# A sparse 3x3 convolution on one core: all input loads issued at the start, every output pair stored in two halves

## The chip, the cores and the metric

The kernel runs on one core of a Trainium2 chip. The metric is the device time of one execution, in microseconds (us); lower is better. The time before is 126.25 us, the median of three runs.

## The reference

The reference is a 3x3 convolution with padding 1 over 16 images. Nine tenths of the weights are zero, but the kernel treats them as dense.

```python
x:      (16, 64, 64, 64)  float32      # batch, c_in, h, w
weight: (128, 64, 3, 3)   float32      # about 90% zeros
x_pad = np.pad(x, ((0,0),(0,0),(1,1),(1,1)))
for b, co, ci, kh, kw:
    output[b, co] += weight[co, ci, kh, kw] * x_pad[b, ci, kh:kh+64, kw:kw+64]
output: (16, 128, 64, 64) float32
```

The input is 16.8 MB, the output 33.6 MB.

## The kernel before, in words

**Pairs.** Images are worked on two at a time. A pair's 2 x 64 input channels fill the 128 partitions of a tile `x{p}` in bf16; there are eight such tiles, one for each pair p = 0 to 7, and none is reused. The loads are issued by GpSimd (the POOL queue), whose DMAs turn fp32 into bf16 on the way (L63 and L68). Only the first 32 rows of pair 0 (`x_head`) come as fp32 through SyncE's queue (L62) and are cast by VectorE and ScalarE (L101). The weights (`w_sb`, L60) come first on that queue.

**When the loads are issued.** Pair 0's second half, pairs 1 to 3 and the first 24 rows of pair 4 are issued at the start. The rest of pair 4 is issued when pair 1's last block has been summed, pair 5 after pair 2, pair 6 after pair 3, and pair 7 in two pieces of 32 rows after pairs 4 and 5 (table `LATER`, L74, calls L197 and L199). Since they stand in GpSimd's own order, they come between its row sums `s` (L169).

**The arithmetic.** Each block is 16 rows of a pair. `direct` (around L164; pair 0's first block alone) uses all nine taps for each row. `twos` takes two rows at a time: GpSimd adds neighbouring rows into `s` (L169), TensorE makes one shared product of `s`, which ScalarE copies out of PSUM into `pc` (L176), and two more products for even and odd rows, to which VectorE adds `pc` while it writes the output tile `o` (L183). All products are matmuls of L150, and a `twos` block has 30 of them.

**The output.** A pair's output is one fp32 tile of 128 partitions x 2 images x 64 rows x 64 columns, 4.2 MB, from a pool `o` of three buffers. SyncE stores a whole pair once its four blocks are written (L207). The last pair alone goes out in two halves of 32 rows (L205). A fourth pair needs the buffer of the first: VectorE's first write to pair p+3 waits until the store of pair p has landed.

**SyncE's eight semaphores.** The DMAs that SyncE issues take eight landing semaphores in turn. An issue whose semaphore was used by an earlier DMA waits until that DMA has landed, and everything behind it in SyncE's order waits too. Five loads of one element (`spare`, L211), issued after pair 1's store, move this rotation on.

In this text 0a and 0b are the first and second 32 rows of pair 0, and so on to 7b.

Of the kernel before, what the change touches and what calls it, by code (L numbers as in the profile page):

```python
# [8 lines left out]
FP32 = mybir.dt.float32  # L9
# [2 lines left out]
SUB = mybir.AluOpType.subtract  # L12

BLOCKS = {p: "TTTT" for p in range(8)}
BLOCKS[0] = "DTTT"  # L20


G0, G1, G2, G21, G01 = range(5)
# [4 lines left out]
def kernel(  # L28
# [6 lines left out]
    nc = tc.nc  # L35

    B, C_IN, H, W = x.shape
    C_OUT, _, KH, KW = weight.shape
    assert (B, C_IN, H, W) == (16, 64, 64, 64) and (C_OUT, KH, KW) == (128, 3, 3)
    NP = B // 2  # L40
    HEAD = 32

    const_pool = ctx.enter_context(tc.tile_pool(name="const", bufs=1))
    x_pool = ctx.enter_context(tc.tile_pool(name="x", bufs=1))
    s_pool = ctx.enter_context(tc.tile_pool(name="s", bufs=3))
    p_pool = ctx.enter_context(tc.tile_pool(name="pc", bufs=4))
    o_pool = ctx.enter_context(tc.tile_pool(name="o", bufs=3))
    psum_pool = ctx.enter_context(
        tc.tile_pool(name="psum", bufs=8, space=bass.MemoryType.PSUM)
    )  # L50
# [4 lines left out]
    def pair(p):  # L55
        return x[2 * p : 2 * p + 2].rearrange("n i h w -> (n i) h w")

    xs = [x_pool.tile([128, H, W], BF16, name=f"x{p}") for p in range(NP)]
# [5 lines left out]
    ident = const_pool.tile([128, 128], BF16, name="ident")  # L64
    make_identity(nc, ident)

    def load(p, a=0, b=H):
        nc.gpsimd.dma_start(out=xs[p][:, a:b, :], in_=pair(p)[:, a:b, :])  # L68

    EARLY, CUT = 4, 24

    LATER = {2: (5,), 3: (6,), 4: (7, 0, 32), 5: (7, 32, 64)}  # L74
    for p in range(1, EARLY):
        load(p)
    load(EARLY, 0, CUT)


    idle_rhs = const_pool.tile([128, 512], BF16, name="idle_rhs")  # L80
    nc.vector.memset(idle_rhs, 0.0)  # L81
# [2 lines left out]
    def keep_busy(n):  # L84
        for _ in range(n):
            nc.tensor.matmul(idle_ps, idle_rhs[:, 0:128], idle_rhs, start=True, stop=True)  # L86

    keep_busy(7)

    w_v = w_sb.rearrange("o (i k) -> o k i", k=KH * KW)
# [66 lines left out]
    def direct(p, o, r0, rows):  # L159
        ps = product(  # L160
            [(xs[p], G1, r0, 1), (xs[p], G0, r0 - 1, 1), (xs[p], G2, r0 + 1, 1)], rows
        )
        nc.scalar.copy(out=o[0][:, r0 : r0 + rows, :], in_=ps[0])  # L163
        nc.vector.tensor_copy(out=o[1][:, r0 : r0 + rows, :], in_=ps[1])  # L164

    def twos(p, o, r0):
        t0 = r0 // 2
        s = s_pool.tile([128, 8, W], BF16, name="s")
        nc.gpsimd.tensor_tensor(  # L169
            out=s, in0=xs[p][:, r0 : r0 + 16 : 2, :], in1=xs[p][:, r0 + 1 : r0 + 16 : 2, :], op=ADD  # L170
        )
        shared = product([(s, G1, 0, 1)], 8)
        pc = []
        for n in range(2):
            c = p_pool.tile([128, 8, W], FP32, name="pc")
            nc.scalar.copy(out=c, in_=shared[n])  # L176
            pc.append(c)
        even = [(xs[p], G21, r0 + 1, 2), (xs[p], G0, r0 - 1, 2)]
        odd = [(xs[p], G01, r0, 2), (xs[p], G2, r0 + 2, 2)]
        for first, terms in ((r0, even), (r0 + 1, odd)):  # L180
            ps = product(terms, 8)
            for n in range(2):
                nc.vector.tensor_tensor(  # L183
                    out=o[n][:, first : r0 + 16 : 2, :], in0=ps[n], in1=pc[n], op=ADD
                )

    for p in range(NP):
        both = o_pool.tile([C_OUT, 2, H, W], FP32, name="o")
        o = [both[:, n] for n in range(2)]
        into = out[2 * p : 2 * p + 2].rearrange("n o h w -> o n h w")  # L190
        last = p == NP - 1
        for blk in range(4):
            r0 = 16 * blk
            if BLOCKS[p][blk] == "T":
                twos(p, o, r0)
                if p == 1 and blk == 3:
                    load(EARLY, CUT, H)  # L197
                elif blk == 3 and p in LATER:
                    load(*LATER[p])  # L199
            else:  # L200
                for r, rows in ((r0, 8), (r0 + 8, 8)):
                    direct(p, o, r, rows)
            if last and blk % 2 == 1:
                rows = slice(r0 - 16, r0 + 16)
                nc.sync.dma_start(out=into[:, :, rows, :], in_=both[:, :, rows, :])  # L205
        if not last:
            nc.sync.dma_start(out=into, in_=both)  # L207
        if p == 1:
            spare = const_pool.tile([1, 5], FP32, name="spare")
            for k in range(5):  # L210
                nc.sync.dma_start(out=spare[:, k : k + 1], in_=weight[0:1, 0, 0, 0:1])  # L211


# [28 lines left out]
```

## Time and profile before

| | us |
|---|---|
| three runs | 125.86, 126.25, 126.41 |
| median | 126.25 |
| span of the profiled execution, first to last instruction | 124.3 |
| what the median has beyond that span | 1.95 |

The page gives the profiled execution by its span; no total of its own is listed beside it, so 1.95 us is taken as what lies around the span.

| engine | busy us | share of the span |
|---|---|---|
| TensorE (PE) | 108.7 | 87% |
| VectorE (DVE) | 82.5 | 66% |
| GpSimd (POOL) | 41.7 | 34% |
| ScalarE (ACT) | 39.0 | 31% |

The DMA share of a stretch is the mean busy share of the core's 16 DMA engines; it can come out a few hundredths above 1 where packets of an engine overlap. GB/s counts what is written at the destination, so a load that turns fp32 into bf16 counts with half of what it reads from HBM. Queue q0 (software) holds GpSimd's loads, queue q1 (hardware) what SyncE issues.

### The profile page before, as it was taken

To read this page: it belongs to the slowest core of one execution; us is meant where nothing else is said; L and a number is where in the kernel's file an instruction comes from. 1 tells how busy PE (TensorE), PEld (TensorE's weight loads), DVE (VectorE), ACT (ScalarE), POOL (GpSimd) and SP (SyncE) were. 2 spreads that over 40 slices of the span, in tenths; PEclk is the share of its full clock that TensorE was granted. 3 is DMA by queue.
4 is the path that set the end of the run, shared out by engine and by line. 5 is a ranking of instruction groups with operands and counts; after the bars stand their busy time and mean duration, and the time that the engine had idled before them with its cause. 6 is when DMAs were issued, how large, how long until landed. Compare 5 with 4: busy or idle time off the path is not lost.

```text
span 124.3 us, 2453 instructions
## 1 busy us (share of the span) xinstructions
PE 108.7 (87%) x989; PEld 57.2 (46%) x989; DVE 82.5 (66%) x135; ACT 39.0 (31%) x71; POOL 41.7 (34%) x47
## 2 busy tenths in 40 slices
PE   6959999999999999999999999999999999970000
PEld 2425555555555555555555555555555555530000
DVE  0353577877787778777877878887877787772000
ACT  4543333333333333333333333333333333330000
POOL 6409333533353335333443335333333320000000
PEclk9999999999999999999999999999999999997555
DMA  4999999999999999999999999999999999999991
GB/s 120 348 220 227 219 213 213 238 411 338 335 392 422 319 316 324 377 340 329 303 385 378 354 380 443 376 349 389 418 422 437 422 427 427 437 427 403 432 414 82
DMA packets 4198, 42.91 MB, mean 345 GB/s; under 512 B 347, under 2 KB 347, under 8 KB 1115
## 3 DMA queue, kind: packets, MB, share of 16 engines
q1 hardware_dynamic: 2746, 34.90, 67.2%
q0 software_dynamic: 1440, 7.86, 30.7%
q8 instruction: 7, 0.11, 0.3%
q14 instruction: 5, 0.03, 0.1%
HBM read 17.07 MB, written 33.55 MB: 407 GB/s over the span
## 4 chain that ended last, share of the span: by engine, by line
PE 82%; DMA 5%; DVE 1%; issue 1%; DVEq 0%; SPq 0%
PE ps L150 82%; DMA x_head<-in_x_dram 5%; DVE o L183 1%; DVEq L237 0%; DVE x L101 0%; SPq L60 0%; DVEq L183 0%
## 5 line engine op out<-in xcount | busy, mean ns | idle before, releaser
L183 DVE TENSOR_TENSOR o<-ps,pc 128x512 f32<-128x512 f32 x124 | 77.8, 686 | 22.1 <-PE ps L150 19.2
L150 PE MATMUL ps<-x,wT 64*128 64x504 bf16 (+3 forms) x780 | 88.8, 373 | 1.3 <-DVE x L101 1.3
L150 PEld LDWEIGHTS <-wT 64*128 64x128 bf16 x966 | 55.2, 94 | 49.5 <-issue 1.7
L169 POOL TENSOR_TENSOR s<-x 128x512 bf16<-128x512 bf16 x31 | 35.6, 1150 | 57.6 <-PE ps L150 41.1
L176 ACT COPY pc<-ps 128x512 f32<-128x512 f32 x62 | 33.3, 589 | 64.0 <-issue 61.8
L150 PE MATMUL ps<-s,wT 64*128 64x512 bf16 (+1 forms) x186 | 25.7, 377 | 0.0
L86 PE MATMUL ps<-idle_rhs 128*128 128x512 bf16 x14 | 4.8, 505 | 1.2 <-DVE idle_rhs L81 1.2
L68 POOL DMA_DIRECT2D x<-in_x_dram x9 | 5.0, 560 | 0.0
L86 PEld LDWEIGHTS <-idle_rhs 128*128 128x128 bf16 x14 | 1.5, 118 | 3.2 <-issue 1.4
L105 DVE CAST w_bf<-w_sb 128x192 bf16<-128x192 f32 (+1 forms) x4 | 1.1, 351 | 2.5 <-DMA w_sb<-in_weight_dram 2.5
L164 DVE COPY o<-ps 128x512 f32<-128x512 f32 x2 | 1.4, 692 | 2.0 <-PE ps L150 2.0
L101 DVE CAST x<-x_head 128x576 bf16<-128x576 f32 x1 | 0.5, 460 | 2.6 <-DMA x_head<-in_x_dram 2.6
L101 ACT CAST x<-x_head 128x576 bf16<-128x576 f32 (+1 forms) x2 | 1.5, 802 | 1.8 <-DMA x_head<-in_x_dram 1.8
L163 ACT COPY o<-ps 128x512 f32<-128x512 f32 x2 | 1.2, 586 | 2.4 <-PE ps L150 2.4
L105 ACT ACT_TABLE_LOAD x1 | 1.3, 1283 | 0.7 <-PEq L226 0.7
L105 ACT CAST w_bf<-w_sb 128x64 bf16<-128x64 f32 (+1 forms) x2 | 0.7, 416 | 1.6 <-DMA w_sb<-in_weight_dram 1.6
L115 DVE TENSOR_TENSOR wT<-ps,wT 128x384 bf16<-128x384 f32 x2 | 1.0, 548 | 0.0
L111 PEld LDWEIGHTS <-w_bf 128*128 128x128 bf16 x9 | 0.5, 97 | 1.0 <-DVE w_bf L105 1.0
L63 POOL DMA_DIRECT2D x<-in_x_dram x1 | 0.7, 693 | 0.8 <-POOLq L226 0.8
L111 PE MATMUL ps<-ident,w_bf 128*128 128x128 bf16 x9 | 0.9, 222 | 0.1
L81 DVE MEMSET idle_rhs<- 128x256 uint32 x1 | 0.3, 272 | 0.9 <-PEq L226 0.9
L126 DVE CAST wT<-ps 128x384 bf16<-128x384 f32 x1 | 0.6, 551 | 0.0
(8 smaller groups left out, 1.9 us busy)
## 6 DMA issues: line engine op xcount, KB each, us to landing
out_dram<-o SPq DMA_DIRECT2D x7, 4096.0 KB, 19.8
x<-in_x_dram POOLq DMA_DIRECT2D x5, 1024.0 KB, 16.8
out_dram<-o SPq DMA_DIRECT2D x2, 2048.0 KB
x<-in_x_dram POOLq DMA_DIRECT2D x3, 512.0 KB, 13.8
x_head<-in_x_dram SPq DMA_DIRECT2D x1, 1024.0 KB, 6.2
x<-in_x_dram POOLq DMA_DIRECT2D x1, 640.0 KB, 14.8
x<-in_x_dram POOLq DMA_DIRECT2D x1, 384.0 KB, 22.3
w_sb<-in_weight_dram SPq DMA_DIRECT2D x1, 288.0 KB
```

Of the source, the lines that this page charges most:

```text
L68: nc.gpsimd.dma_start(out=xs[p][:, a:b, :], in_=pair(p)[:, a:b, :])
L86: nc.tensor.matmul(idle_ps, idle_rhs[:, 0:128], idle_rhs, start=True, stop=True)
L101: copy(out=xs[0][:, a:b, :], in_=x_head[:, a:b, :])
L105: copy(out=w_bf4[:, g, a:b, :], in_=w_v[:, k : k + b - a, :])
L111: nc.tensor.matmul(wps[:, j, :], src, ident, start=True, stop=True)
L115: nc.vector.tensor_tensor(out=wT[:, g], in0=wps, in1=wT[:, G1], op=SUB)
L150: nc.tensor.matmul(ps[n][:, lo:hi, c_lo:c_hi], tap(g, kw, n), src[q, a:b:step, c_lo + kw - 1 : c_hi + kw - 1], start=(i == 0), stop=(i == ...
L163: nc.scalar.copy(out=o[0][:, r0 : r0 + rows, :], in_=ps[0])
L164: nc.vector.tensor_copy(out=o[1][:, r0 : r0 + rows, :], in_=ps[1])
L169: nc.gpsimd.tensor_tensor(out=s, in0=xs[p][:, r0 : r0 + 16 : 2, :], in1=xs[p][:, r0 + 1 : r0 + 16 : 2, :], op=ADD)
L176: nc.scalar.copy(out=c, in_=shared[n])
L183: nc.vector.tensor_tensor(out=o[n][:, first : r0 + 16 : 2, :], in0=ps[n], in1=pc[n], op=ADD)
```

## The change

All input loads are issued at the start, each pair in one piece. Every pair is stored in two halves of 32 rows, each once its two blocks are written, instead of only the last pair. The pool of three rotating output buffers becomes three tiles of fixed names, taken in turn (`outs[p % 3]`), so that the waits are tracked by region: a write to the first half of pair p+3 waits for the store of the first half of pair p alone. The one-element loads after pair 1 are six instead of five.

```diff
-    o_pool = ctx.enter_context(tc.tile_pool(name="o", bufs=3))
+    o_pool = ctx.enter_context(tc.tile_pool(name="o", bufs=1))
...
-    EARLY, CUT = 4, 24
-
-    LATER = {2: (5,), 3: (6,), 4: (7, 0, 32), 5: (7, 32, 64)}
-    for p in range(1, EARLY):
-        load(p)
-    load(EARLY, 0, CUT)
+    for p in range(1, NP):
+        nc.gpsimd.dma_start(out=xs[p], in_=pair(p))
...
+    outs = [o_pool.tile([C_OUT, 2, H, W], FP32, name=f"o{k}") for k in range(3)]
     for p in range(NP):
-        both = o_pool.tile([C_OUT, 2, H, W], FP32, name="o")
+        both = outs[p % 3]
...
             if BLOCKS[p][blk] == "T":
                 twos(p, o, r0)
-                if p == 1 and blk == 3:
-                    load(EARLY, CUT, H)
-                elif blk == 3 and p in LATER:
-                    load(*LATER[p])
...
-            if last and blk % 2 == 1:
+            if p in HALVES and blk % 2 == 1:          # HALVES = range(8)
                 rows = slice(r0 - 16, r0 + 16)
                 nc.sync.dma_start(out=into[:, :, rows, :], in_=both[:, :, rows, :])
-        if not last:
+        if p not in HALVES:
             nc.sync.dma_start(out=into, in_=both)
         if p == 1:
-            spare = const_pool.tile([1, 5], FP32, name="spare")
-            for k in range(5):
+            spare = const_pool.tile([1, SPARES], FP32, name="spare")      # SPARES = 6
+            for k in range(SPARES):
                 nc.sync.dma_start(out=spare[:, k : k + 1], in_=weight[0:1, 0, 0, 0:1])
```

In the program as built, SyncE's order after the change is: weights, `x_head`, 0a, 0b, 1a, 1b, six spares, 2a, 2b, and so on to 7b. By the rotation of the eight semaphores the fifth spare waits for the landing of 0a, the sixth for 0b, 2a for 1a, 2b for 1b, 6a for 2a, 6b for 2b, 7a for 3a and 7b for 3b; 3a to 5b wait for spares. TensorE's and ScalarE's instructions and their order are as before.

More of the change, by code (lines that the diff above doesn't have):

```diff
@@ L20 @@
 BLOCKS[0] = "DTTT"
+HALVES = range(8)
+SPARES = 6
 G0, G1, G2, G21, G01 = range(5)
@@ L65 @@
     make_identity(nc, ident)
-    def load(p, a=0, b=H):
-        nc.gpsimd.dma_start(out=xs[p][:, a:b, :], in_=pair(p)[:, a:b, :])
-    EARLY, CUT = 4, 24
-    LATER = {2: (5,), 3: (6,), 4: (7, 0, 32), 5: (7, 32, 64)}
-    for p in range(1, EARLY):
-        load(p)
-    load(EARLY, 0, CUT)
+    for p in range(1, NP):
+        nc.gpsimd.dma_start(out=xs[p], in_=pair(p))
     idle_rhs = const_pool.tile([128, 512], BF16, name="idle_rhs")
@@ L185, in twos @@
                 )
+    outs = [o_pool.tile([C_OUT, 2, H, W], FP32, name=f"o{k}") for k in range(3)]
     for p in range(NP):
-        both = o_pool.tile([C_OUT, 2, H, W], FP32, name="o")
+        both = outs[p % 3]
         o = [both[:, n] for n in range(2)]
         into = out[2 * p : 2 * p + 2].rearrange("n o h w -> o n h w")
-        last = p == NP - 1
         for blk in range(4):
```

## The prediction

> **What bounds the kernel now.** I read the busy rows of the page first, then the slices and the account of HBM, then the chain, then the windows, the two DMA queues in single stretches, and SyncE's waits.
>
> ```profile
> span 124.3 us, 2453 instructions
> PE 108.7 (87%) x989; PEld 57.2 (46%) x989; DVE 82.5 (66%) x135; ACT 39.0 (31%) x71; POOL 41.7 (34%) x47
> PE   6959999999999999999999999999999999970000
> DMA  4999999999999999999999999999999999999991
> HBM read 17.07 MB, written 33.55 MB: 407 GB/s over the span
> PE 82%; DMA 5%; DVE 1%; issue 1%; DVEq 0%; SPq 0%
> ```
>
> The first row and the chain name TensorE. But the chain's shares add up to 89%: it stops at VectorE's last add, 112.6 us, and does not carry the last 12 us. In the slices TensorE is idle there and the DMA engines are not; they are at 9 in every slice but the first and the last. The windows (TensorE, weight loads, VectorE, ScalarE, GpSimd, clock, DMA share, GB/s) say how full, and SyncE's waits say what ended last:
>
> ```profile
> 8.00:24.00 16.00, 16.00 (x152) 8.58 (x153) 10.65 (x18) 6.42 (x12) 8.43 (x8) 1.00 1.03 214
> 90.00:106.00 16.00, 16.00 (x154) 8.53 (x151) 12.52 (x21) 5.32 (x11) 4.19 (x4) 1.00 1.01 428
> 106.00:113.00 7.00, 5.23 (x50) 2.58 (x46) 5.14 (x9) 1.69 (x4) 0.00 (x0) 1.00 0.98 418
> 113.00:121.00 8.00, 0.00 (x0) 0.00 (x0) 0.00 (x0) 0.00 (x0) 0.00 (x0) 0.53 1.01 428
> 121.00:124.30 3.30, 0.00 (x0) 0.00 (x0) 0.00 (x0) 0.00 (x0) 0.00 (x0) 0.50 0.24 99
> SPq L237 <- DMA out_dram<-o: 10.0, 3, 4.8
> ```
>
> From 8 to 24 us only loads run: 214 GB/s written as bf16 are 428 read. From 90 to 121 only stores run: 428 too. So the 16 engines move 428 GB/s of HBM traffic either way, and 17.07 + 33.55 = 50.62 MB need 118.3 us. The rest of the span: the first 4 us move 0.6 MB and lose 2.6 us; the mixed stretch from 24.3 to 89.4 moves 27.7 MB (queue q1 19.79 MB, q0 3.89 counted twice, 0.10 of instructions) at 425 GB/s and loses 0.46; the last 3.3 us (0.33 MB, engines finishing one after another) lose 2.5. Together 123.9 of 124.3. Both TensorE and DMA look full, but only DMA sets the end: the last half is issued at 112.6 and needs 4.9 us (2.10 MB / 428), yet the span ends at 124.3, because the store before it is still in the queue. TensorE has some 4 to 5 us to spare.
>
> So the question for each edit is whether it changes the bytes (no), the rate, or leaves the DMA engines without work.
>
> **The change part by part.**
>
> *Loads issued early.* Before the first row sum GpSimd issues three more loads of 560 ns (the page's row for L68), 1.7 us, from 4.6 to 6.3 us. Next on GpSimd is that sum, which starts at 9.04 because it waits for ScalarE's cast: hidden, 0; without that cover at most 1.7 us at a place where TensorE is not what ends last. Later five issues of 0.57 us vanish ahead of row sums on an engine that is 34% busy: 0.
>
> *Loads in whole pairs.* Pairs 4 and 7 came in two pieces. The queue lines of two stretches (packets, MB, share of 16 engines):
>
> ```profile
> q1 hardware_dynamic: 142, 2.33, 57.0%
> q0 software_dynamic: 112, 0.92, 43.9%
> ```
>
> This is 40 to 50 us, with whole-pair loads: 0.439 x 10 us x 16 / 112 = 627 ns for one 8 KB packet. From 78 to 86 us, where halves of pair 7 load:
>
> ```profile
> q0 software_dynamic: 120, 0.49, 29.9%
> ```
>
> 0.299 x 8 x 16 / 120 = 319 ns for 4 KB, so two cost 638. An engine has 8 rows of each pair: 8 x 11 ns = 0.09 us for pair 7, about the same for pair 4. I take -0.2 us, ends -0.4 and 0.
>
> *Stores in halves.* SyncE issues 16 stores instead of 9, 0.4 us each, on a queue that waits 90 us: 0. Their packets are 8 KB instead of 16 KB. The stretch from 113 to 121 holds only halves (7a, 7b) and shows 428 GB/s, as does 90 to 106 with whole pairs; from 114 to 120 alone it is 426. 29.4 MB x (1/426 - 1/428) = 0.3 us. I take +0.1, ends 0 and +0.3.
>
> The Trainium skill ("DMA: Bandwidth & Descriptors", section "Anatomy of one DMA — SWDGE (gpsimd) path") speaks against this edit: about 2.0 us fixed for every DMA. Seven more stores at that price one after another would make 14 us, some 140 us in all. The windows disagree: 106 to 121 us holds the seams between pair 6, 7a and 7b at shares of 0.98 and 1.01, so a fixed part lies beside the store ahead of it.
>
> *A different mixture.* Half 0a is complete when VectorE ends the second block of pair 0 at 16.5 us (the timeline has its four adds from 13.98, 2.51 long); whole pair 0 was issued at 23.03. From then on stores and loads share. Loads alone would end at 2 + 17.07 / 0.428 = 42 us, so 24 us of them are left at 17.6. In the lines above, 142 store packets went against 112 load packets, 1.27 to 1. With store packets of 309 ns (113 to 121 us) stores get 1.27 x 309 / (1.27 x 309 + 627) = 0.385 of the time, and the loads end at about 17.6 + 24.4 / 0.615 = 57 us: 39 us of mixture instead of 65. Its rate is not in the trace with these sizes. Nearest: 420 GB/s from 40 to 50 us (2.33 + 2 x 0.92 + 0.03 MB; whole-pair loads, large stores), 425 over all the mixture, 419 at its slowest (38 to 53 us: 349 written, and 1.05 MB of loads counted again), 428 for no loss. The loss against 428 is 39 x 8 / 428 = 0.73 us at 420, 0.82 at 419, 0 at 428; the old mixture's 0.46 goes. I take 420, the same loads: +0.3, ends -0.5 and +0.4.
>
> The skill's same page, section "Queues, rings and completion order", says that an engine turns between queues packet by packet. The 1.27 to 1 is near that. Equal turns would give the stores 0.33 instead of 0.385 and the loads an end at 54; the sum stays, since the same bytes go either way.
>
> *The new waits.* 2a now waits for 1a's landing, though its data is there at 42 (SyncE issued pair 1's store at 35.78; a half takes 6.4). Behind it on SyncE stand 2b (48.6) and 3a (55). Whatever the shares, when 1a has landed, at most all loads and three halves have gone: 42 + 3 x 4.9 = 57 us, up to 2 more for the slowest engine (the engines end between 121 and 123.4). Between 1a's landing and 2a's first bytes I allow 2.2 us: the weights' 0.29 MB, issued at 0.74, were there at 3.67, 0.7 us of it transfer. 1b, 4.9 us, is in the queue then, and covers it. The same holds for 2b behind 2a. From there on stores are ready before their turn: by 65 us 3a and 3b are complete. So the engines always have work: 0. Without that cover a gap would cost up to 2.2 us at each of the two waits.
>
> *Output tiles.* VectorE's first write to 4a, at 62.0, waits for 1a (57 to 59); 5a at 74.8 waits for 2a (some 67 to 69). 3 and 5 us of margin; a miss takes TensorE's spare 4 to 5 us first. The additional waits of VectorE on its own earlier adds (a semaphore instruction is 21 ns) lie in its 42 idle us: 0.
>
> Sum: -0.2 + 0.1 + 0.3 = +0.2 us on the span, 124.5. With the 1.95 that the median has beyond the span: 126.4. Ends of the terms: -0.9 and +0.7; what the engines' finishing order does (2 us between first and last now) can add half a us to either side.
>
> **The rivals.**
>
> *Faster: the mixture was the loss.* Loading in one go leaves pure stores after 57 us. If the new mixture runs at 425 or better, the terms make -0.3 to -0.9; if the engines also finish closer together (half of the 2 us spread is 0.5 on average), some 125.3. For it: 419 from 38 to 53 us, where whole-pair loads run beside stores, against 427 from 66 to 90 us with smaller ones. Against it: 0.46 us is all that the old mixture loses.
>
> *Slower: small store packets beside large load packets.* From 17.6 to 57 us every turn now moves 8 KB out for 16 KB in. If each change of direction costs, the rate falls below anything in the trace: at 408 GB/s the 16.5 MB cost 1.2 us more than at 420, 127.6. It decides from about 414 on (+0.6 us in all). For it: more packets change hands per MB; against it: 4 to 8 us, 8 KB packets on both queues, 0.67 + 2 x 0.51 MB, makes 422.
>
> *The halves do not leave as they are done.* 2a and 2b are held for 15 us by the waits above, so the change does less than it says; as the queue is never empty, the price is 0 and this belongs to the forecast.
>
> **How the numbers follow.** About 0.5%, 0.6 us, is what a measurement of this kernel can tell from no change. The forecast (same bytes, full DMA, 125.5 to 127.0) has 0.54: 0.46 within, 0.04 on each side. The faster rival has 0.22, the slower 0.24. This makes faster 0.26, same 0.46, slower 0.28. The range takes both rivals' values: 125.2 to 127.6.
>
> **What would show it.** Right: DMA share 1.0 from 4 to 121 us, no loads after some 57 us, 428 GB/s after that, SyncE's last wait on a store, the last half issued at about 112.6. Wrong: a share under 0.95 anywhere between 55 and 70 us (the waits of 2a and 2b), VectorE waiting for a store at 49, 62 or 75 us, or a mixture under 414 or above 427 GB/s.

## The result and the profile after

The changed kernel takes 127.62 us (median of four runs, 127.54 to 127.77) against 126.19 before: 1.0115 times as long, 95% interval 1.0084 to 1.0146. So it is slower by 1.4 us, just past the upper end of the predicted range (127.6). The profiled execution took 127.64 us, 125.9 of it span; 1.8 us lie around it, much as before. Medians here are over all runs of a kernel, while the ratios leave out runs that were disturbed, so the two don't always divide.

The page of the changed kernel, the rows that answer to those of before:

```profile
span 125.9 us, 2502 instructions
PE 109.5 (87%) x989; PEld 57.2 (45%) x989; DVE 82.6 (66%) x135; ACT 38.9 (31%) x71; POOL 40.7 (32%) x45
PE   6999999999999999999999999999999999920000
DMA  4999999999999999999999999999999999999980
GB/s 118 357 217 229 208 211 221 279 297 281 289 268 302 292 279 284 286 344 419 422 422 430 422 422 427 432 424 414 430 430 427 414 427 432 422 422 437 430 357 16
HBM read 17.07 MB, written 33.55 MB: 402 GB/s over the span
```

TensorE ends at 110.9 us (before 111.2), the bytes are the same, and the DMA engines are at 9 from the second slice to the last but two: still the bound, and never without work. The GB/s row shows the mixture ending in the eighteenth slice (53.5 to 56.7 us), and pure stores after it. But the traffic over the span is 402 GB/s instead of 407. The windows (TensorE, weight loads, VectorE, ScalarE, GpSimd, clock, DMA share, GB/s) of the changed kernel, with two stretches of the end, say where:

```profile
18.00:20.00 2.00, 2.00 (x22) 1.08 (x20) 1.43 (x3) 1.07 (x2) 1.07 (x1) 1.00 1.09 188
92.00:110.00 18.00, 18.00 (x172) 9.54 (x170) 13.81 (x23) 6.44 (x12) 3.46 (x3) 1.00 1.01 425
113.00:121.00 8.00, 0.00 (x0) 0.00 (x0) 0.00 (x0) 0.00 (x0) 0.00 (x0) 0.65 1.02 430
121.00:123.00 2.00, 0.00 (x0) 0.00 (x0) 0.00 (x0) 0.00 (x0) 0.00 (x0) 0.50 0.65 274
123.00:125.00 2.00, 0.00 (x0) 0.00 (x0) 0.00 (x0) 0.00 (x0) 0.00 (x0) 0.50 0.04 16
```

and of the kernel before:

```profile
92.00:110.00 18.00, 18.00 (x172) 9.60 (x168) 13.89 (x23) 6.45 (x12) 3.45 (x3) 1.00 1.01 430
121.00:123.00 2.00, 0.00 (x0) 0.00 (x0) 0.00 (x0) 0.00 (x0) 0.00 (x0) 0.50 0.39 164
123.00:125.00 2.00, 0.00 (x0) 0.00 (x0) 0.00 (x0) 0.00 (x0) 0.00 (x0) 0.50 0.00 0
```

Three things are to be seen. From 18 to 20 us only loads land, at 188 GB/s instead of 214, though the share is full: each load packet takes longer. From 92 to 110 the halves go out at 425 GB/s where whole pairs went at 430, but at 430 again from 113 on, when nothing is computed. (A window counts a packet where it starts. With each packet shared out over its time, the three rates are 424.9, 429.0 and 428.0.) And after 123 us a share of 0.04 of 16 engines over 2 us is left, 1.3 us of a single engine: the trace's landing marks of the last store have 15 engines in by 123.46 us and the last at 124.97.

Those marks split the loss. In the last store's 16 landings the first engine went from 121.30 to 122.01 us, the median from 122.33 to 122.95, the last from 123.44 to 124.97. So the first and the median engine lost 0.6 to 0.7 us, and the last one 1.5, some 0.8 more. The fifteenth of the 16 lost only 0.2 (123.24 to 123.46): the end is set by one engine.

The traffic of both traces, summed over time by parts of packets, says when the shared part is lost. Against before, the changed kernel is 0.06 us ahead at 18 us, 0.5 behind at 24, 0.3 at 57 and 0.6 from 110 to 121 (bytes behind, at 428 GB/s).

SyncE's waits in the changed kernel:

```profile
SPq L189 <- DVE o L171: 75.4, 14, 14.6
SPq L189 <- DMA out_dram<-o: 13.8, 2, 9.4
SPq L195 <- DMA out_dram<-o: 12.8, 1, 12.8
SPq L221 <- DMA out_dram<-o: 11.8, 3, 4.8
```

The third line and the second are the rotation's waits: the sixth spare for 0b (landed at 50.3 us), then 2a for 1a and 2b for 1b. They hold SyncE for 26.6 us in all, and, as the DMA row shows, no engine ran dry for it.

### The profile page after: what moved, and what is told of

Read it like the earlier page. It is cut to its first block, busy times and chain, and to the rows that moved or that the text cites. A ratio compares the mean times of both kernels' runs of the same rounds, so it can differ in the third digit from the quotient of the medians.

```text
span 125.9 us, 2502 instructions
## 1 busy us (share of the span) xinstructions
PE 109.5 (87%) x989; PEld 57.2 (45%) x989; DVE 82.6 (66%) x135; ACT 38.9 (31%) x71; POOL 40.7 (32%) x45
## 4 chain that ended last, share of the span: by engine, by line
PE 81%; DMA 5%; DVE 1%; issue 1%; DVEq 1%; SPq 0%
PE ps L138 81%; DMA x_head<-in_x_dram 5%; DVE o L171 1%; DVEq L221 0%; DVE x L89 0%; SPq L59 0%; DVEq L171 0%
## 5 line engine op out<-in xcount | busy, mean ns | idle before, releaser
L157 POOL TENSOR_TENSOR s<-x 128x512 bf16<-128x512 bf16 x31 | 35.6, 1152 | 58.2 <-PE ps L138 41.8
L67 POOL DMA_DIRECT2D x<-in_x_dram x7 | 3.7, 560 | 0.0
L62 POOL DMA_DIRECT2D x<-in_x_dram x1 | 0.7, 696 | 0.8 <-POOLq L210 0.8
L112 ACT CAST wT<-ps 128x384 bf16<-128x384 f32 x1 | 0.5, 479 | 0.4 <-PE ps L99 0.4
```

The source lines that it names most:

```text
L67: nc.gpsimd.dma_start(out=xs[p], in_=pair(p))
L157: nc.gpsimd.tensor_tensor(out=s, in0=xs[p][:, r0 : r0 + 16 : 2, :], in1=xs[p][:, r0 + 1 : r0 + 16 : 2, :], op=ADD)
```

## The experiments

Three theories stood at the start, S, H and E; a fourth, O, took the place of E after the first four runs. **E**: loads issued in one heap cost wherever they meet stores. **O**, the onset: the moment when a store first meets queued loads costs, since both slow down. **H**, halves: small store packets cost by themselves. **S**, the slow engine: in stretches where only stores run beside compute one DMA engine falls behind, and the change made these stretches longer (54 us instead of 22). The ratios are to the kernel before, measured beside each run.

| run | median us | ratio | 95% interval |
|---|---|---|---|
| changed kernel | 127.62 | 1.0115 | 1.0084 to 1.0146 |
| whole_stores | 127.66 | 1.0134 | 1.0105 to 1.0162 |
| old_loads | 127.77 | 1.0150 | 1.0117 to 1.0183 |
| late_loads | 127.27 | 1.0098 | 1.0069 to 1.0128 |
| no_spares | 127.95 | 1.0158 | 1.0129 to 1.0188 |
| before_pair4_whole | 126.65 | 1.0058 | 1.0036 to 1.0080 |
| before_heap_at_23 | 126.63 | 1.0068 | 1.0039 to 1.0097 |
| before_halves_4_to_7 | 126.34 | 1.0038 | 1.0014 to 1.0063 |
| whole_stores_aligned | 127.12 | 1.0091 | 1.0072 to 1.0110 |
| halves_empty_onset | 129.36 | 1.0266 | 1.0240 to 1.0292 |
| before_quarters_4_to_7 | 127.26 | 1.0117 | 1.0102 to 1.0133 |
| before_fixed_tiles | 126.49 | 1.0025 | 0.9998 to 1.0052 |
| before_trickle | 126.24 | 1.0020 | 0.9997 to 1.0044 |
| halves_fed_onset | 129.69 | 1.0267 | 1.0219 to 1.0315 |
| changed_centre_tap | 126.18 | 1.0001 | 0.9968 to 1.0035 |
| before_centre_tap | 126.30 | 1.0014 | 0.9982 to 1.0045 |

**Each half of the change alone.**

```diff
-HALVES = range(8)
+HALVES = (7,)                      # whole_stores: loads early, whole pairs stored
```

> All loads early as in the changed kernel, but whole pairs stored again (only pair 7 in halves): the load part of the change alone. Theory S (in stretches where only stores run, one DMA engine moves about 3% less than the others, and the change made these stretches longer, 54 us instead of 22): loads end near 62 us, some 48 us of store-only beside compute, so 0.03 x 26 = +0.8 us, about 127.0 us. Theory H (the halves cost by themselves: smaller packets, more seams): 126.2 us, as before. Theory E (loads issued in one heap cost by themselves, wherever they meet stores): about 127.5 us.

```diff
+    for piece in [(1,), (2,), (3,), (4, 0, 24)]: load(*piece)
+    # old_loads: the rest of 4 after pair 1, 5 after 2, 6 after 3, 7 in two after 4 and 5
```

> Halves, fixed tiles and six spares as in the changed kernel, but the old load schedule: the store part of the change alone. Theory S: half stores give way faster to loads, so the stretches with both are short here too; about 127.2 us. Theory H: about 127.5 us. Theory E: 126.2 us.

Both are as slow as the changed kernel, 127.66 and 127.77 us: neither half is innocent, and the two losses don't add. No theory had said so alone; S came nearest, with 127.0 and 127.2. whole_stores also held a cost of its own, met again below.

```diff
+    LATER = {(2, 0): (4,), (3, 1): (5,), (4, 1): (6,), (5, 2): (7,)}    # late_loads; 1 to 3 at the start
```

> The changed kernel with pairs 4 to 7 loaded singly and later than in either kernel (issued near 27, 42, 55 and 70 us). Theory S: the sum of the store-only stretches is as in the changed kernel with its halves, so 127.2 to 127.6 us. Theory H: 127.5 us. Theory E: 126.2 us or a little less.

127.27 us: a little below the changed kernel, with intervals that overlap, and not by what would make the early loads the cause. Its first store still met loads, as pair 3 was in the queue (193 GB/s from 18 to 20 us in the windows), and its halves went at 425 GB/s from 92 to 110 us.

**The held stores.**

```diff
-        if p == 1:
-            spare = ...             # no_spares: the six one-element loads are gone
```

> The changed kernel without the six one-element loads: no store waits for 0a, 0b, 1a or 1b through the rotation, so 2a is issued near 42 us and not 60. Theories S, H and E: 127.6 us, no change, since the DMA engines never ran dry. Theory W (holding 2a and 2b back costs): 126.5 us or less.

Theory W, that the held stores cost, falls. Without the spares 2a is issued at 41.8 us instead of 60, and yet 7b lands at 124.86 us, against 124.97. The 0.3 us by which the run is slower come after that: its span ends 1.27 us after the landing, the changed kernel's 0.90. SyncE's closing waits go through the semaphores in a fixed order; without the spares the last store uses the second of the eight, and the waits for the others follow its landing. That is what the spares are for, and the next run tests it:

```diff
-SPARES = 6
+SPARES = 5                         # whole_stores_aligned
```

> The run with early loads and whole stores again, with five one-element loads instead of six. With six, the last store used a semaphore that SyncE's closing waits check first, and eight more checks (0.5 us) followed its landing at 124.25; with five it is checked last. Theory T (these closing checks): 0.4 us less than with six, about 127.2; the remaining +1.1 us are O and S. If T is wrong: 127.6.

127.12 us, 1.0091 instead of 1.0134. SyncE's closing waits of whole_stores and then of whole_stores_aligned:

```profile
SPq L221 <- DMA out_dram<-o: 10.1, 1, 10.1
```

```profile
SPq L221 <- DMA out_dram<-o: 9.7, 2, 4.9
```

With six spares there is one wait, on the last store, and all the other waits come behind it (span 125.6); with five the last store is waited for last (span 125.2). In both the landing is the same, 124.25 and 124.31 us. So early loads alone cost about 0.9%, not 1.3%.

**Onset.**

```diff
-    EARLY, CUT = 4, 24
+    EARLY, CUT = 4, 64              # before_pair4_whole
```

> The kernel before with one edit: pair 4 is loaded whole at the start, so some 3 us of loads are still queued when the first store arrives (before, the loads end about when it does). In the first four runs the DMA rate fell to 374 to 397 GB/s in the 6 us after a store met a full load queue; before it was 412. Theory O (this meeting costs): +0.3 to +0.4 us, about 126.5. Theory S (slow engine in store-only stretches): 126.1, since those stretches hardly change. Theory H: 126.1.

+0.58%, somewhat more than expected. The window of this run from 25 to 27 us (the second line is whole_stores_aligned in the same stretch):

```profile
25.00:27.00 2.00, 2.00 (x22) 1.06 (x20) 1.27 (x3) 1.07 (x2) 1.15 (x1) 1.00 0.98 152
```

```profile
25.00:27.00 2.00, 2.00 (x22) 0.89 (x20) 1.27 (x3) 1.07 (x2) 1.15 (x1) 1.00 1.00 135
```

The first store was issued at 22.7 and 22.9 us. Loads go on at full rate until 25, and then at 152 and 135 GB/s instead of 214 for 2 us, with hardly a store packet beside them (the first ones start at 26.7 and 27.1 us). Against 214 that is 0.6 and 0.7 us lost. In the changed kernel the queues from 16.3 to 20 us, after 0a was issued at 16.28:

```profile
DMA packets 105, 0.73 MB, mean 197 GB/s; under 512 B 16, under 2 KB 16, under 8 KB 16
## 3 DMA queue, kind: packets, MB, share of 16 engines
q0 software_dynamic: 105, 0.73, 105.2%
```

No packet of queue q1: the first one starts at 20.1, 3.8 us after the issue. In the kernel before it starts 1.3 us after (23.03 to 24.31); there the loads were just running out. Its small dip comes later, at 27 to 29 us, when the rest of pair 4 starts. Counted on all bytes by parts of packets, the dips lose 0.43 us in the changed kernel (18 to 21 us: 398, 355, 348 GB/s of HBM traffic, against 428) and 0.18 before (407, 372).

Two runs were to take the onset away from the changed kernel:

```diff
+    for piece in [(1,), (2, 0, 40)]: load(*piece)     # halves_empty_onset
+    # rest of pair 2 after the third block of pair 1, pair 3 after the fourth
```

> The run with late loads again, with the loads at the start cut to pairs 0, 1 and 40 rows of pair 2, so that the load queue is empty when the first half is issued at 16.3 us; the rest of pair 2 follows at 17, pair 3 at 23.5. In the first eight runs a store issued to a full queue had its first packets 3.8 to 4.4 us after issue, not 1.3, and the load packets of that time took up to 900 ns instead of 625. Theory O: the dip goes and with it 0.3 to 0.5 us: 0.4% less than late_loads, that is 0.6% over before. If the meeting is not the cause: 1.0% over before, as late_loads.

```diff
+    for piece in [(1,), (2, 0, 48)]: load(*piece)     # halves_fed_onset
+    # rest of pair 2 after the second block of pair 1, pair 3 after the third
```

> As halves_empty_onset, but without the gaps it had: there the rest of pair 2 was issued only at 20 us and the DMA rate fell to 88 GB/s at 16 to 17 us, 165 at 22 to 23. Now 48 rows of pair 2 come at the start, the last 16 about 17 us, pair 3 about 20 us. Theory O: no stretch of slow load packets at 18 to 21 us, 0.3 to 0.5 us less than late_loads (1.0% over before): 0.6 to 0.7% over before. If the meeting of stores and queued loads is not the cause: 1.0%.

Both missed: 2.7% slower than before. Windows of halves_empty_onset, then of halves_fed_onset:

```profile
16.00:17.00 1.00, 1.00 (x12) 0.51 (x10) 0.27 (x2) 0.56 (x2) 0.79 (x1) 1.00 0.08 10
22.00:24.00 2.00, 2.00 (x23) 1.05 (x21) 1.40 (x3) 1.01 (x2) 1.67 (x2) 1.00 0.89 107
```

```profile
16.00:17.00 1.00, 1.00 (x12) 0.52 (x10) 0.35 (x1) 0.35 (x1) 1.00 (x2) 1.00 0.76 195
22.00:26.00 4.00, 4.00 (x42) 2.13 (x40) 2.89 (x5) 1.88 (x4) 2.00 (x2) 1.00 0.94 166
```

The first ran dry at 16 us. In the second the rest of pair 2, issued at 16.5 beside a running store, had its first packet at 21.4, 4.9 us after the issue. In halves_empty_onset it was 2.4 us (19.97 to 22.37), and there the last packet of 0a had just started. When 0a was done, 0b had to start anew: no store packet starts between 23.5 and 26.0 us in the second run, and between 22.3 and 24.6 in the first. So it is not shown that the changed kernel could be had without its onset; what it costs is shown by the dip and by before_pair4_whole.

**Halves.**

```diff
-            if last and blk % 2 == 1:
+            if p >= 4 and blk % 2 == 1:      # before_halves_4_to_7; spares 2
```

> The kernel before with pairs 4 to 7 stored in halves (before: 7 alone), and two one-element loads instead of five, so that the last store takes the semaphore that the closing checks come to last, as before. Theory H: three more pairs in halves; the engines' landings in the changed kernel lie 4.91 us apart for a half and were 9.74 for a whole pair before, so 3 x 0.08 = +0.25 us, 126.3; if halves were the whole loss, 3/7 of 1.5 = +0.6. Theories O and S: 126.1.

```diff
-            if last and blk % 2 == 1:
-                rows = slice(r0 - 16, r0 + 16)
+            if p >= 4:                       # before_quarters_4_to_7; spares 2
+                rows = slice(r0, r0 + 16)
```

> The kernel before with pairs 4 to 7 stored in four pieces of 16 rows (4 KB packets), closing semaphore as before. Halves for the same pairs were +0.4%. Theory H: the loss goes on with the size of the packets and the number of stores: +0.8% or more, 126.9 and up. If halves cost only by what they do to the mixture with the loads (theory S alone): +0.4% as with halves, or less.

+0.38% and +1.17%: theory H holds, and the loss grows with smaller packets. The windows from 92 to 110 us, first with halves, then with quarters:

```profile
92.00:110.00 18.00, 18.00 (x172) 9.61 (x170) 13.79 (x23) 6.45 (x12) 3.46 (x3) 1.00 1.01 426
```

```profile
92.00:110.00 18.00, 18.00 (x172) 8.21 (x168) 13.78 (x23) 6.44 (x12) 3.46 (x3) 1.00 1.03 419
```

430, 426, 419 GB/s for packets of 16, 8 and 4 KB, with compute beside them; by parts of packets 429.0, 425.5 and 418.5. Smaller packets also mean more stores, and the packets themselves tell the two apart. On an engine that nothing disturbs, one packet of 16 KB follows another after 607 ns, one of 8 KB after 306, one of 4 KB after 156, with no gap where one store ends and the next begins. So 16 KB take 607, 612 and 624 ns: 0.8% more in halves, 2.8% in quarters. The price lies in the packets, not in the number of stores.

**The tiles.**

```diff
+    outs = [o_pool.tile([C_OUT, 2, H, W], FP32, name=f"o{k}") for k in range(3)]
-        both = o_pool.tile([C_OUT, 2, H, W], FP32, name="o")
+        both = outs[p % 3]                   # before_fixed_tiles
```

> The kernel before with three fixed output tiles instead of the rotating pool: the remaining part of the change alone. All theories: no change (0.0%), since VectorE's additional waits are on its own earlier work. Theory R (region tracking costs): +0.2% or more.

The interval takes in no change (0.9998 to 1.0052), and the profiled span was 124.1 us, below that of before. No cost of the tiles is shown; a quarter of a per cent can't be excluded.

**The slow engine.**

```diff
-    LATER = {2: (5,), 3: (6,), 4: (7, 0, 32), 5: (7, 32, 64)}
+    LATER = {}                               # before_heap_at_23:
+                    for q in range(EARLY + 1, NP): load(q)     # after the rest of pair 4
```

> The kernel before with pairs 5, 6 and 7 issued together with the rest of pair 4 at 23.5 us, just after the first store: the start of the first store is untouched, but the loads end near 65 us instead of 89, so the store-only stretch beside compute grows from 22 to about 46 us. Theory S: 0.03 x 24 = +0.7 us, 126.8. Theory O: 126.1, or 126.4 if the queue now met is as bad. Theory H: 126.1.

+0.68%, as S says, with loads ending at 68 us. In its trace the last landings are spread over 2.85 us (120.75 to 123.61), before over 2.15. The profiled execution itself was only 0.2 us longer than that of before, while the ratio makes 0.86, so the size rests on the times.

```diff
+    LATER = {(2, 3): (5, 0, 32), (3, 1): (5, 32, 64), (3, 3): (6, 0, 32), (4, 1): (6, 32, 64),
+             (4, 3): (7, 0, 16), (5, 1): (7, 16, 32), (5, 3): (7, 32, 48), (6, 1): (7, 48, 64)}
```

> The kernel before with pairs 5 and 6 loaded in two pieces and pair 7 in four, issued one after another from 36 to 81 us: smaller load packets take a smaller share beside the stores, so the loads last until about 95 us instead of 89 and fill the gaps between. Theory S: the store-only stretch beside compute falls from 22 to 15 us, -0.2 us (0.2% faster than before), less 0.2 us for the smaller load packets: 0 to -0.2%. If S is wrong: +0.1 to +0.2%.

1.0020 (0.9997 to 1.0044): no gain. The run neither supports S nor speaks clearly against it.

The packets of the two traces show the slow engine itself. In the changed kernel one unbroken chain of 164 packets, each starting as the one ahead ends, runs from 58.1 to 111.3 us with 324 ns from packet to packet instead of 306, 6% more, and it is this engine that lands last. Its 164 x 18 ns make 3.0 us, close to the spread of 2.95. Before, such a chain has 38 packets, from 88.2 to 112.6 us, with 641 ns instead of 607: 1.3 us. So the engine is 5 to 6% slower, not the 3% that the theories were given. In both traces the long packets stop soon after TensorE does (110.9 and 111.2 us). So the last test takes work from TensorE:

```diff
-KW_ORDER = (1, 0, 2)
+KW_ORDER = (1,)                          # changed_centre_tap, before_centre_tap
```

These two kernels leave out six of the nine taps, so they compute another result; loads and stores stay as they are.

> The changed kernel with the centre column of taps alone: a third of TensorE's matmuls, the same bytes. The slow DMA engine of the changed kernel was slow as long as TensorE ran (to about 111 us) and not after. Theory S1 (TensorE's work or what is recorded of it slows that engine): the spread between the first and the last engine at the last landing falls from 2.95 us to about 2, and the time to about 126.8 us. Theory S2 (the engine is slow for a cause of its own, or through VectorE's writes): spread 2.9, time 127.6 us.

> The kernel before with the centre column of taps alone. Theory S1: spread from 2.15 to about 1.7 us, 125.8 us. Theory S2: no change, 126.1 us. Theories O and H speak for no change either: the bytes and pieces are the same, and the DMA engines remain the bound.

The changed kernel falls from 127.6 to 126.18 us, and its spread from 2.95 to 1.52 us. Its windows:

```profile
92.00:110.00 18.00, 2.84 (x17) 0.78 (x13) 6.95 (x12) 1.55 (x3) 0.00 (x0) 0.66 1.01 428
121.00:123.00 2.00, 0.00 (x0) 0.00 (x0) 0.00 (x0) 0.00 (x0) 0.00 (x0) 0.50 0.44 184
123.00:125.00 2.00, 0.00 (x0) 0.00 (x0) 0.00 (x0) 0.00 (x0) 0.00 (x0) 0.50 0.00 0
```

The straggler is gone (0.00 after 123 us), and the same halves go at 428 instead of 425 GB/s: compute beside them slows them, as it does whole pairs (430.4 in before_centre_tap, 429.0 before, by parts of packets). The loads and stores, their pieces and their order are those of the changed kernel. S1 holds, with a fall of 1.4 us where 0.8 was expected. TensorE ends at 95.4 us here, so the slow stretch is shorter as well as weaker.

Two rivals are left to S1. The other engines had less to do from 92 to 110 us as well, so one of them might be the cause. From 75 to 88 us they had more (the changed kernel, then changed_centre_tap):

```profile
75.00:88.00 13.00, 13.00 (x126) 6.92 (x122) 10.25 (x18) 4.30 (x8) 4.62 (x4) 1.00 1.02 427
75.00:88.00 13.00, 10.84 (x58) 3.58 (x55) 13.00 (x23) 6.13 (x11) 5.93 (x6) 0.87 1.01 427
```

With VectorE, ScalarE and GpSimd all busier and less than half of the matmuls, what the long packets take beyond 309 ns falls from 0.78 to 0.52 us. That goes with TensorE and against the others. And the instructions that the kernel fetches fall from 0.11 to 0.03 MB (queue q8 of the pages); a fetch of 16 KB holds one engine for some 0.9 us. But the changed kernel's slow chain runs on through the fetches at 70.7, 85.2 and 98.6 us, so they are on other engines.

The kernel before does not gain with it (126.30), which S1 alone would not say; its spread falls from 2.15 to 1.78. Its trace has why: with less compute its first store is ready at 18.3 us instead of 23.0 and meets loads that were to end at 24.

```profile
20.00:22.00 2.00, 1.71 (x10) 0.64 (x10) 2.00 (x5) 1.16 (x2) 1.26 (x2) 1.00 1.01 139
```

139 GB/s instead of 214 in this stretch: from 20 to 24 us it falls 1.2 us behind the kernel before (by parts of packets), the onset once more.

No run beat the kernel before.

## Why the prediction was wrong

**The bound was right.** The reading that the DMA engines and not TensorE set the end holds: bytes the same, no engine without work, TensorE ending at 110.9 us with time to spare. So did the schedule: the loads ended at 57.0 us (predicted 57), 1a landed at 59.9 (57 to 59), 2a was issued at 60.0, and neither that wait nor the output tiles reached the end; no_spares shows it for the wait.

**The term of the halves was mis-sized.** The prediction took 428 GB/s for 8 KB packets from 113 to 121 us and added 0.1 us (at most 0.3). That window has no compute in it, while the 428 of whole pairs, from 90 to 106, has. Beside compute the halves run at 424.9 and whole pairs at 429.0 (by parts of packets): over the 54 us from 57 to 111 some 0.5 us. From 57 to 110 us the changed kernel falls back by 0.34 us, less than that, as the kernel before still had loads in its mixture until 89 us (426.6 GB/s from 62 to 90). The right packets were read in the wrong surroundings.

**The finishing order was treated as noise.** This is the largest miss. "Half a us to either side" was allowed for it, and nothing in the sum. It has a sign: one engine is 5 to 6% slower where only stores run beside TensorE's work, some 22 us before and 54 after, and the spread grew by 0.8 us. The trace of before held it already, as an engine with long packets until TensorE ended; the windows' means over 16 engines hide it. changed_centre_tap shows that it goes with TensorE's work.

**The onset was missing.** The prediction put the loss of the mixture into its rate. That rate was well met: 24 to 57 us moved 5.34 + 2 x 4.29 + 0.03 MB, 423 GB/s, against 420 taken. What it did not see is the start. It let the mixture begin at 17.6 us, 1.1 us after 0a would be complete, and put the start itself at nothing. But a store issued to a full load queue waits 3.8 us, to 20.1, and the loads slow down meanwhile: 0.43 us against 0.18. In the kernel before, the loads issued at the start run out about as the first store comes (24.3 us); the prediction gave this no price.

Term by term: up to 57 us, where the prediction had -0.2 for the whole pieces and +0.3 for the mixture, 0.34 us are lost, mostly at the onset; from 57 to 110 us, where it had +0.1, another 0.34; and the one engine, where it had 0, adds 0.8. That is 1.5, as the span grew from 124.3 to 125.9. The parts tried alone come to more: 0.73 us for an onset, 0.86 for the heap, 0.48 for three pairs of halves. They overlap, and how is not settled.

**The rivals.** The slower one had the sign and, by chance, the size (127.6). Its mechanism, a mixture under 414 GB/s, did not happen. The faster one fell: it asked for a mixture at 425 or better and for engines that finish closer together; the mixture ran at 423, and the engines finished further apart.

## What to carry to other kernels

Where DMA is the bound, take a packet's price from a stretch with the same compute beside it, and look at each engine's last landing, not only at the mean share: one engine of sixteen sets the end. Starting a second queue beside a full one cost 0.4 to 0.7 us here, and 1.2 in one run, so the moment of the first store decides how much to load ahead of it. And a full DMA row of nines is no proof that nothing can be lost: the traffic over the span (402 against 407 GB/s) is.

## What was not expected of the hardware

A queue that becomes active beside a busy one starts late: 3.8 us from the start of the issue to the first packet for a store beside queued loads (1.3 when the loads run out), 2.4 and 4.9 us for a load beside a running store. In between the busy queue's own packets take up to some 950 ns instead of 625. The Trainium skill ("DMA: Bandwidth & Descriptors", section "Specifications") gives about 0.6 us to the first byte on the path that SyncE's stores take. The program's first DMA, with nothing beside it, had its first packet 1.0 us after the start of its issue (0.74 to 1.76) and 0.6 after the issue's end; the store's 3.8 us are far above both.

One DMA engine was 5 to 6% slower as long as TensorE worked. The same page (section "Latency and other measured facts") says that engines 7 and 15 are usually slower, and guesses at the ring that GpSimd's DMAs fetch their descriptors from. The records don't name the engine. The guess doesn't fit here: the slowness shows after the last load, shrinks when TensorE has a third of its matmuls, and ends soon after them. Whether the matmuls do it, or what the profiler records of them, stays open.

SyncE's closing waits cost 0.4 us more when the last store uses a semaphore that they reach early.
